# A load moved to another queue, a fetch moved ahead and a token shift rewritten, in the mixer of a hybrid decoder layer

## The chip, the cores and the metric

The kernel runs on one core of one Trainium2 chip. The metric is the device time of one execution in microseconds; the time of a kernel is the median of several runs. The profile is one execution, taken by the hardware profiler: TensorE (PE, with its weight loads as PEld), VectorE (DVE), ScalarE (ACT), GpSimd (POOL) and SyncE (SP), which here only issues DMAs.

## The reference

One decoder layer in float32, with 1024 tokens of 1024 channels: a SwiGLU half-step, a mixer, a SwiGLU half-step, each between two RMS norms. The mixer projects the normed input with one matrix and feeds three branches: RWKV-7 time mixing, sliding-window attention and cross-attention into 256 memory tokens; their outputs are gated, added and projected.

The change concerns the RWKV branch. Its 14 blocks of 128 projected channels go through the token shift:

```
p_prev = pad(p, one token)[:-1]
p = p + (p_prev - p) * mu          # mu: one number for each channel
r, k, v, wd, ad, gd = split(p)
```

From these come a decay, and vectors a and b, and then the recurrence over the tokens for 8 heads of 64 channels:

```
sa = state @ a_t
state = state * w_t + sa * b_t + v_t * k_t
y_t = state @ r_t
```

## The kernel before, in words

**Layout.** Activations lie with channels on the 128 partitions and tokens along the free axis. Tokens are worked in two halves of 512 (`TH`), the size of a PSUM bank. Every large product is done three times (`mm3`, lines 374 to 379): weight and input are each split into a rounded high part and a rest (float32r), and high times high, high times rest and rest times high are added in one bank. A weight strip is loaded by SyncE (`raw`, line 291, five buffers), its high part is made by ScalarE (line 300) and its rest by VectorE (line 302). `prefetch` makes up to eight such operands ahead of their use.

**Who sets the order.** The program is written as a sequence; a planner (the tile framework's scheduler) then lays down a fixed order for every engine from priorities, dependences and its own estimate of costs. `high_priority(offset=...)` moves what stands in it ahead: `lead` is 300, `urgent` is 1000. `issue_after` and `keep_in_program_order` fix an order by hand. Each engine and each DMA queue then takes its instructions strictly in that order, and waits at one whose inputs or buffers aren't ready. A pool with `bufs=2` has two buffers; the third user waits until the first is released, which for a tile that is stored to DRAM means until its store is complete.

**Stages of the mixer.**

1. `rwkv_prep` (line 1002): for each of four pairs of heads the blocks k, r and v are projected (16 times 3 matmuls for a block over both halves) and shifted by `rwkv_block` (line 953); before them come the blocks 12 (`low`) and 13 (`gd`). Four of the 14 blocks (`MIX_FIRST`) were projected already beside the first half-step and wait in `raw` tiles. A `raw` tile has eight columns ahead of its 1024 tokens, the last of them zero, so that columns 7 onward are the tokens shifted by one. For the other ten blocks ScalarE copies both banks into `raw` (line 963). Then VectorE subtracts (line 965) and multiplies and adds (line 966). The results go on to the decay, the norm of the keys (`normed`, `head_sums`, bank name `ss`), the products of keys (`gram`, bank name `ab`) and the planes that are stored in `pk_d` for each chunk of 64 tokens.
2. `win_pair` (line 1407): seven pairs of the other input blocks (attention and gates), each pair in seven products (`b11`, `b21`, `t2`, `t1`, `t3`, `b22`, `t4`) over sums of inputs and sums of weights, which are added in the banks `px`, `py` and `pz`. A pair fills two output tiles, `first` and `second`, of a pool with two buffers; VectorE (line 1433) or ScalarE (lines 1436 and 1438) writes their four halves, and SyncE stores them (line 1455). The half of `second` that the product `t3` gives is read from `px`, into which `t4` is added afterwards.
3. Beside the first pair, `rwkv_invert` (line 1146) inverts, on VectorE, the two triangular 32 by 32 blocks on the diagonal of each of the 128 matrices of 64 by 64, and stores them in `inv_d` (line 1162) and one of them turned in `turn_d` (line 1165).
4. Beside the fifth and sixth pair, `rwkv_corner` (line 1167) makes the remaining 32 by 32 corner: half = up times turned, corner = half times low. Three blocks are loaded with rows and matrices exchanged (line 1177): `up` from `ab_d`, `turned` from `turn_d` and `low` from `inv_d`, each in four DMAs of 128 KB on SyncE with `urgent` priority. Their 512 small matmuls (line 1185) are given out in eight lumps, one behind each product of a pair. ScalarE's queue stores the corner in `inv_d` (line 1191).
5. `chunk_fetch` (line 1193) loads, for one chunk, its planes (`f`, line 1196) and its inverse (`dinv`, two DMAs, line 1198). Those of chunks 0 and 1 are written in the program ahead of the last pair (line 1789), with no priority of their own, after the pool of the corner's tiles has been closed.
6. `rwkv_chain` (line 1201) runs the recurrence over 16 chunks with small matmuls (line 1211). The gate blocks 10 and 11 (`gate_block`, bank name `pgate`) and later the generator `filling` give TensorE work between its steps.

After that come the norm of the branch, both attentions, the branch products and the second half-step.

Of the kernel before, what the change touches and what calls it, by code (L numbers as in the profile page):

```python
# [11 lines left out]
F32 = mybir.dt.float32  # L12
F32R = mybir.dt.float32r
I32 = mybir.dt.int32
ALU = mybir.AluOpType
ACT = mybir.ActivationFunctionType
AXX = mybir.AxisListType.X

P = 128
T = 1024  # L20
TH = 512
# [40 lines left out]
NC_ = T // C  # L62
H = C // 2
# [21 lines left out]
VOFF = {}  # L85
# [146 lines left out]
class Builder:  # L232
# [665 lines left out]
    def mixer_consts(self, cp):  # L898
        nc, io = self.nc, self.io
        V = nc.vector  # L900
        self.lora = cp.tile([P, 512], F32, name="lora")
        nc.scalar.dma_start(self.lora, io["lora"])
        self.g_up = cp.tile([P, 512], F32, name="g_up")
        nc.scalar.dma_start(self.g_up, io["g_up"])
        self.center = cp.tile([P, C], F32, name="center")
        for q in (0, 64):
            V.tensor_scalar(self.center[q : q + 64], self.ident[q : q + 64, q : q + 64], 1.0 / C, None, ALU.subtract)
        self.bones_r = cp.tile([P, P], F32R, name="bones_r")
        bones = self.bones_r.bitcast(F32)
        V.memset(bones, 0.0)  # L910
        for q in (0, 64):
            V.memset(bones[q : q + 64, q : q + 64], 1.0)
        self.gmask = cp.tile([P, 2, C], F32, name="gmask")
        nc.gpsimd.memset(self.gmask, 1.0)
        for q in (0, 64):
            for i, op in ((0, ALU.is_gt), (1, ALU.is_ge)):
                m = self.gmask[q : q + 64, i, :]
                nc.gpsimd.affine_select(m, m, [[1, C]], op, 0.0, base=0, channel_multiplier=-1)
        self.neg_kk = cp.tile([P, NPAIR], F32, name="neg_kk")
        o = VOFF["rwkv_k_k"][0]  # L920
        V.tensor_scalar(self.neg_kk, self.vecs[:, o : o + 4], -1.0, None, ALU.mult)
        self.half_ka, self.half_w0, self.half_a0 = (cp.tile([P, NPAIR], F32, name="half_" + n) for n in ("ka", "w0", "a0"))
        for t, n in ((self.half_ka, "rwkv_k_a"), (self.half_w0, "rwkv_w0"), (self.half_a0, "rwkv_a0")):
            o = VOFF[n][0]
            V.tensor_scalar(t, self.vecs[:, o : o + 4], 0.5, None, ALU.mult)
        self.one_ka = cp.tile([P, NPAIR], F32, name="one_ka")
        V.tensor_scalar(self.one_ka, self.half_ka, -1.0, 1.0, ALU.mult, ALU.add)
        self.half_gb = cp.tile([P, 24], F32, name="half_gb")
        o = VOFF["gate_b"][0]
        V.tensor_scalar(self.half_gb, self.vecs[:, o : o + 24], 0.5, None, ALU.mult)  # L930
        self.ln_half = cp.tile([P, 1], F32, name="ln_half")
        V.memset(self.ln_half, float(np.log(0.5)))
        self.sinks = cp.tile([P, 8], F32, name="sinks")
        nc.scalar.dma_start(self.sinks, io["sinks"])
        self.rope_c = cp.tile([P, 2], F32, name="rope_c")
        nc.scalar.dma_start(self.rope_c, io["rope_c"])
        self.half_pi = cp.tile([P, 1], F32, name="half_pi")
        V.memset(self.half_pi, float(np.pi / 2))
        self.wmask = cp.tile([P, P], F32, name="wmask")
        nc.gpsimd.memset(self.wmask, 0.0)  # L940
        nc.gpsimd.affine_select(self.wmask, self.wmask, [[-1, P]], ALU.is_ge, NEG, base=0, channel_multiplier=1)
        self.is_own = cp.tile([P, P], F32, name="is_own")
        nc.gpsimd.memset(self.is_own, 1.0)
        nc.gpsimd.affine_select(self.is_own, self.is_own, [[1, P]], ALU.is_ge, 0.0, base=0, channel_multiplier=-1)
        before = cp.tile([P, P], F32, name="is_before")
        nc.gpsimd.memset(before, 1.0)
        nc.gpsimd.affine_select(before, before, [[1, P]], ALU.is_gt, 0.0, base=0, channel_multiplier=-1)
        self.is_before = before.bitcast(I32)
        self.gn_eps = cp.tile([P, 64], F32, name="gn_eps")[:, :1]
        V.memset(self.gn_eps, GN_EPS)  # L950


    def rwkv_block(self, f, u, out, within={}):

        nc = self.nc
        if self.first:
            raw = self.first.pop(0)
        else:
            raw = self.raw_tile()
            ps = {h: self.psum("pr") for h in (0, 1)}  # L960
            self.project(self.strip("win", f), u, ps, within)
            for h in (0, 1):
                nc.scalar.copy(raw[:, 8 + h * TH : 8 + (h + 1) * TH], ps[h])
        cur, before = (self.chunked(raw[:, i : i + T], out) for i in (8, 7))
        nc.vector.tensor_tensor(out, before, cur, ALU.subtract)
        self.mixed = nc.vector.scalar_tensor_tensor(out, out, self.vec("rwkv_mu", f), cur, ALU.mult, ALU.add)

    def raw_tile(self, low=False):
        raw = self.rawpool.tile([P, T + 8], F32, tag="rawl" if low else "raw", name="raw", bufs=1 if low else len(MIX_FIRST) - 1)
# [197 lines left out]
    def rwkv_corner(self, pool, ab_d, inv_d, turn_d):  # L1167

        nc = self.nc
        flat = lambda d: d.rearrange("c p q s t -> (c p q) s t")  # L1170
        groups = [slice(g * H, (g + 1) * H) for g in range(P // H)]
        up, turned, low, half, corner = (pool.tile([P, H, H], F32, name="i" + n, bufs=1) for n in ("up", "turned", "low", "half", "corner"))
        urgent = lambda: self.tc.high_priority(offset=self.urgent)
        with urgent():
            for t, d in ((up, flat(ab_d)[:, :H, H:]), (turned, turn_d), (low, flat(inv_d)[:, H:, H:])):
                for g in groups:
                    nc.sync.dma_start(t[g], d[g].rearrange("i s t -> s i t"))
        for w, x, out in ((up, turned, half), (half, low, corner)):
            for a in range(0, H, H // 4):
                if a % (H // 2) == 0:  # L1180
                    ps = self.psum("corner").rearrange("p (i t) -> p i t", t=H)
                with urgent():
                    for i in range(a, a + H // 4):
                        for g in groups:
                            mm = self.tc.keep_in_program_order(nc.tensor.matmul(ps[g, i % (H // 2)], w[g, i], x[g, i], start=True, stop=True))
                    if a % (H // 2):
                        nc.scalar.copy(out[:, a - H // 4 : a + H // 4], ps)
                yield mm
        with urgent():
            for g in groups:  # L1190
                nc.scalar.dma_start(flat(inv_d)[g, :H, H:].rearrange("i s t -> s i t"), corner[g])
# [549 lines left out]
    def mixer(self, u, cp, close_raws, att_d, gate_d, km_d, vm_d):  # L1741
        nc, tc, io = self.nc, self.tc, self.io
        pk_d = tc.dram_tile([NC_, P, NPAIR, 5 * C], F32, name="pk_d")
        ab_d = tc.dram_tile([NC_, NPAIR, 2, C, C], F32, name="ab_d")
        inv_d = tc.dram_tile([NC_, NPAIR, 2, C, C], F32, name="inv_d")
# [18 lines left out]
        with tc.tile_pool(reuse_waits="tile", name="gates", bufs=2) as gp:  # L1764
            out = lambda: gp.tile([P, T], F32, tag="gate", name="att", bufs=2)
# [20 lines left out]
                assert next(lumps, None) is None  # L1786
            chunks = contextlib.ExitStack()
            early = chunks.enter_context(tc.tile_pool(reuse_waits="tile", name="chunks", bufs=2))
            fetched = [self.chunk_fetch(early, c, pk_d, inv_d) for c in (0, 1)]
            self.win_pair(len(WIN_PAIRS) - 1, fs, out, att_d, gate_d)  # L1790
            over.close()
            with chunks, tc.tile_pool(reuse_waits="tile", name="chain", bufs=2) as pool:
# [275 lines left out]
```

## Time and profile before

| | us |
|---|---|
| time, median of three runs | 2256.55 |
| lowest and highest of them | 2255.40, 2257.11 |
| the profiled execution, its time | 2257.27 |
| its span, first to last instruction | 2255.6 |
| granted TensorE clock, mean over the span | 0.997 of full |
| ScalarE busy | 1028.9 |
| GpSimd busy | 58.8 |
| DMA, moved over the span | 431.90 MB |

All positions below are microseconds from the span's start. A row of the order of time gives start, duration, engine, line, operation, output<-inputs, size and count; in brackets stands how long the engine was idle before it and which instruction released it. A row of a list of waits gives the waiter and whom it waited for, then the total in us, the number of waits and the longest. A row of the groups by line gives the operation with its count, shortest/median/longest duration in ns, and the first and last start. SPq and ACTq are DMA issues on the queues of SyncE and ScalarE. The granted clock is a share of TensorE's full clock.

### The profile page before, as it was taken

To read this page: it belongs to the slowest core of one execution; us is meant where nothing else is said; L and a number is where in the kernel's file an instruction comes from. 1 tells how busy PE (TensorE), PEld (TensorE's weight loads), DVE (VectorE), ACT (ScalarE), POOL (GpSimd) and SP (SyncE) were. 2 spreads that over 40 slices of the span, in tenths; PEclk is the share of its full clock that TensorE was granted. 3 is DMA by queue.
4 is the path that set the end of the run, shared out by engine and by line. 5 is a ranking of instruction groups with operands and counts; after the bars stand their busy time and mean duration, and the time that the engine had idled before them with its cause. 6 is when DMAs were issued, how large, how long until landed. Compare 5 with 4: busy or idle time off the path is not lost.

```text
span 2255.6 us, 34511 instructions
## 1 busy us (share of the span) xinstructions
PE 2227.7 (99%) x12304; PEld 1832.2 (81%) x12304; DVE 1642.0 (73%) x2761; ACT 1028.9 (46%) x1933; POOL 58.8 (3%) x114
## 2 busy tenths in 40 slices
PE   8999999999999999999999999999999999999998
PEld 6888888888887788877878887788888888888887
DVE  6988767766698887863667577794898886656576
ACT  6523333454556654444355454444663223345451
POOL 0000000000000000000330000000000000000000
PEclk9999999999999999999999999999999999999999
DMA  8565666686665356464538877564565552347663
GB/s 292 174 202 169 202 210 214 229 294 205 191 210 188 120 150 204 155 169 153 158 95 276 270 252 250 185 202 142 174 214 176 194 189 100 114 164 249 205 196 121
DMA packets 279132, 431.90 MB, mean 191 GB/s; under 512 B 58512, under 2 KB 96912, under 8 KB 278704
## 3 DMA queue, kind: packets, MB, share of 16 engines
q1 hardware_dynamic: 266160, 409.96, 56.0%
q10 hardware_dynamic: 12800, 19.73, 2.7%
q8 instruction: 97, 1.59, 0.3%
q14 instruction: 75, 0.61, 0.1%
HBM read 292.75 MB, written 135.79 MB: 190 GB/s over the span
## 4 chain that ended last, share of the span: by engine, by line
PE 51%; DMA 1%; DVE 1%; ACT 1%; issue 0%; SPq 0%; DVEq 0%; ACTq 0%
PE px L377 4%; PE px L379 4%; PE px L378 4%; PE po L377 3%; PE po L378 3%; PE po L379 3%; PE pgate L377 2%; PE pgate L378 2%; PE pgate L379 2%; PE pz L377 2%; PE pz L379 2%; PE pz L378 2%; PE pb L377 2%; PE pb L378 2%; PE pb L379 2%; PE pw L378 1%
## 5 line engine op out<-in xcount | busy, mean ns | idle before, releaser
L300 ACT CAST w_hi<-w_raw 128x512 fp32r<-128x512 f32 x608 | 376.2, 620 | 725.0 <-PE px L378 189.9
L302 DVE TENSOR_TENSOR w_lo<-w_raw,w_hi 128x512 fp32r<-128x512 f32 x608 | 417.3, 688 | 191.0 <-ACT w_hi L300 171.7
L379 PE MATMUL po<-u,w_lo 128*128 128x512 f32 (+1 forms) x476 | 180.9, 380 | 0.0
L378 PE MATMUL po<-u,w_hi 128*128 128x512 f32 (+1 forms) x476 | 180.9, 380 | 0.0
L377 PE MATMUL po<-u,w_hi 128*128 128x512 f32 (+1 forms) x476 | 180.9, 380 | 0.0
L377 PE MATMUL px<-u,w_hi 128*128 128x512 f32 x380 | 147.9, 389 | 0.8 <-DVE km L1596 0.8
L377 PE MATMUL pz<-u,w_hi 128*128 128x512 f32 x380 | 148.1, 390 | 0.0
L378 PE MATMUL px<-u,w_hi 128*128 128x512 f32 x380 | 147.9, 389 | 0.0
L379 PE MATMUL px<-u,w_lo 128*128 128x512 f32 x380 | 147.8, 389 | 0.0
L379 PE MATMUL pz<-u,w_lo 128*128 128x512 f32 x380 | 147.8, 389 | 0.0
L378 PE MATMUL pz<-u,w_hi 128*128 128x512 f32 x380 | 147.8, 389 | 0.0
L377 PE MATMUL px<-f,w_hi 128*128 128x512 f32 x352 | 137.1, 390 | 0.0
L379 PE MATMUL px<-f,w_lo 128*128 128x512 f32 x352 | 137.0, 389 | 0.0
L378 PE MATMUL px<-f,w_hi 128*128 128x512 f32 x352 | 136.9, 389 | 0.0
L486 DVE TENSOR_TENSOR u<-hid,u 128x512 fp32r<-128x512 f32 x114 | 78.3, 690 | 44.7 <-ACT u L485 43.7
L378 PEld LDWEIGHTS po<-u,w_hi 128*128 128x128 f32 x476 | 89.5, 188 | 17.2
L379 PEld LDWEIGHTS po<-u,w_lo 128*128 128x128 f32 x476 | 89.5, 188 | 17.0
L377 PE MATMUL pgate<-u,w_hi 128*128 128x512 f32 x256 | 103.3, 403 | 0.0
L377 PEld LDWEIGHTS po<-u,w_hi 128*128 128x128 f32 x476 | 89.5, 188 | 16.8
L378 PE MATMUL pgate<-u,w_hi 128*128 128x512 f32 x256 | 101.0, 395 | 0.0
L485 ACT CAST u<-hid 128x512 fp32r<-128x512 f32 x114 | 70.6, 620 | 65.0 <-DMA hid<-form_d 54.2
L379 PE MATMUL pgate<-u,w_lo 128*128 128x512 f32 x256 | 100.3, 392 | 0.0
(453 smaller groups left out, 5162.1 us busy)
## 6 DMA issues: line engine op xcount, KB each, us to landing
w_raw<-in_ffn_in SPq DMA_DIRECT2D x224, 256.0 KB
hid<-form_d SPq DMA_DIRECT2D x154, 256.0 KB
w_raw<-in_win SPq DMA_DIRECT2D x112, 256.0 KB
form_d<-g SPq DMA_DIRECT2D x88, 256.0 KB
w_raw<-ffn_sum_d SPq DMA_DIRECT2D x88, 256.0 KB
form_d<-h SPq DMA_DIRECT2D x66, 256.0 KB
w_raw<-in_ffn_out SPq DMA_DIRECT2D x66, 256.0 KB
first_d<-first SPq DMA_DIRECT2D x48, 256.0 KB
```

What stands on the lines that cost most here:

```text
L300: self.nc.scalar.copy(hi, x)
L302: self.split_last = self.nc.vector.tensor_tensor(lo, x, hi.bitcast(F32), ALU.subtract)
L377: mm(out, wh, xh, start=first, stop=False, **kw)
L378: mm(out, wh, xl, start=False, stop=False, **kw)
L379: self.last_mm = mm(out, wl, xh, start=False, stop=last, **kw)
L485: self.nc.scalar.copy(hi, x)
L486: self.nc.vector.tensor_tensor(lo, x, hi.bitcast(F32), ALU.subtract)
```

## The change

Three edits in the mixer.

- In `rwkv_corner` the block `low` is loaded by GpSimd's queue, in eight DMAs of half the size in place of four on SyncE's. `up` and `turned` stay where they were.
- The fetch of chunks 0 and 1 is given `urgent` priority (1000).
- The token shift is written as out = (1 - mu) * cur + mu * before. A new constant tile `rest_mu` holds 1 - mu. ScalarE writes (1 - mu) * cur into the output, in two halves straight out of the PSUM banks, or in one copy out of `raw` for the four blocks that were projected earlier; VectorE then does one multiply-and-add with the shifted columns. The copies into `raw` stay.

```diff
...
+        self.rest_mu = cp.tile([P, 14], F32, name="rest_mu")
+        o = VOFF["rwkv_mu"][0]
+        V.tensor_scalar(self.rest_mu, self.vecs[:, o : o + 14], -1.0, 1.0, ALU.mult, ALU.add)
...
     def rwkv_block(self, f, u, out, within={}):
         nc = self.nc
+        rest = self.rest_mu[:, f : f + 1]
         if self.first:
             raw = self.first.pop(0)
+            nc.scalar.activation(out, self.chunked(raw[:, 8 : 8 + T], out), ACT.Copy, scale=rest)
         else:
...
                 nc.scalar.copy(raw[:, 8 + h * TH : 8 + (h + 1) * TH], ps[h])
-        cur, before = (self.chunked(raw[:, i : i + T], out) for i in (8, 7))
-        nc.vector.tensor_tensor(out, before, cur, ALU.subtract)
-        self.mixed = nc.vector.scalar_tensor_tensor(out, out, self.vec("rwkv_mu", f), cur, ALU.mult, ALU.add)
+                part = out[:, h * NC_ // 2 : (h + 1) * NC_ // 2] if len(out.shape) == 3 else out[:, h * TH : (h + 1) * TH]
+                nc.scalar.activation(part, self.chunked(ps[h], part), ACT.Copy, scale=rest)
+        self.mixed = nc.vector.scalar_tensor_tensor(out, self.chunked(raw[:, 7 : 7 + T], out), self.vec("rwkv_mu", f), out, ALU.mult, ALU.add)
...
             for t, d in ((up, flat(ab_d)[:, :H, H:]), (turned, turn_d), (low, flat(inv_d)[:, H:, H:])):
                 for g in groups:
-                    nc.sync.dma_start(t[g], d[g].rearrange("i s t -> s i t"))
+                    if t is not low:
+                        nc.sync.dma_start(t[g], d[g].rearrange("i s t -> s i t"))
+                        continue
+                    for a in (0, H // 2):
+                        nc.gpsimd.dma_start(t[g, a : a + H // 2], d[g][a : a + H // 2].rearrange("i s t -> s i t"))
...
-            fetched = [self.chunk_fetch(early, c, pk_d, inv_d) for c in (0, 1)]
+            with tc.high_priority(offset=self.urgent):
+                fetched = [self.chunk_fetch(early, c, pk_d, inv_d) for c in (0, 1)]
             self.win_pair(len(WIN_PAIRS) - 1, fs, out, att_d, gate_d)
```

## The prediction

> **What bounds the kernel now.** I read the page first, then the busy time of each engine by stage, then the list of waits of TensorE, and last the order of time around the one long wait.
>
> ```profile
> span 2255.6 us, 34511 instructions
> PE 2227.7 (99%) x12304; PEld 1832.2 (81%) x12304; DVE 1642.0 (73%) x2761; ACT 1028.9 (46%) x1933; POOL 58.8 (3%) x114
> ```
>
> TensorE works 2227.7 of 2255.6 us. The change takes no matmul away and adds none, so all that it can win is TensorE's idle time, 27.9 us, and time in which its clock was lower. The change touches the mixer only, so the next view is the busy time of the stages that it touches (columns: stretch, its length, then busy time and count of PE, PEld, DVE, ACT and POOL, then granted clock, DMA share, GB/s).
>
> ```profile
> 722.00:900.00 178.00, 175.77 (x1002) 142.27 (x1002) 151.24 (x171) 96.48 (x149) 1.05 (x10) 1.00 0.52 153
> 1000.00:1022.00 22.00, 18.64 (x286) 14.71 (x286) 7.03 (x12) 7.41 (x13) 0.00 (x0) 0.92 0.67 143
> 1060.00:1190.00 130.00, 126.83 (x2029) 104.60 (x2028) 79.54 (x181) 61.82 (x134) 48.08 (x74) 1.00 0.43 134
> ```
>
> The three rows are the preparation of the recurrence (where the token shift runs), the corner, and the chain of chunks. TensorE is idle there for 178.00 - 175.77 = 2.2 us, 22.00 - 18.64 = 3.4 us and 130.00 - 126.83 = 3.2 us. Only in the corner is the clock under 1.00. The waits of TensorE name the causes:
>
> ```profile
> PE px L377 <- DVE att L1433: 3.4, 1, 3.4
> PE z L1211 <- DVE sv L1302: 1.8, 2, 1.1
> PE ss L993 <- DVE n_lo L486: 1.3, 1, 1.3
> ```
>
> The 3.4 us is the corner's, the 1.8 us is two waits in the chain, the 1.3 us one wait in the preparation. The order of time on TensorE at the first:
>
> ```profile
> 1012.57 0.75 PE L1185 MATMUL corner<-iturned,iup 32*32 32x32 f32 x64
> 1016.68 0.65 PE L377 MATMUL px<-mix_form,w_hi 128*128 128x512 f32 x1 [3.36 <-DVE att L1433]
> ...
> 1020.43 0.39 PE L377 MATMUL px<-mix_form,w_hi 128*128 128x512 f32 x1
> 1020.65 0.39 PE L378 MATMUL px<-mix_form,w_hi 128*128 128x512 f32 x1
> ```
>
> ```profile
> 1017.00:1018.00 1.00, 1.00 (x4) 0.71 (x4) 0.00 (x0) 0.43 (x1) 0.00 (x0) 0.50 0.00 0
> ```
>
> After the wait, nine matmuls take 1020.43 - 1016.68 = 3.75 us; the pitch of the next two is 0.22 us, at which nine take 2.0. The granted clock in that stretch is 0.50. So the wait costs 3.36 us of idle time and 1.7 us of slow work, 5.1 us in all. (The Trainium skill, "TensorE: Matmul & The Clock Gate", Part 1 on the clock gate, says that the clock halves after an idle window of about 3.4 us; the trace agrees as far as one wait of 3.36 us can show. By that page a shorter wait would cost no slow work.)
>
> Why was VectorE late? Its own order of time, and the queue of SyncE:
>
> ```profile
> 1012.68 0.69 DVE L1433 TENSOR_TENSOR att<-pz,part 128x512 f32<-128x512 f32 x1 [2.47 <-PE pz L379]
> 1013.29 0.68 DVE L302 TENSOR_TENSOR w_lo<-w_raw,w_hi 128x512 fp32r<-128x512 f32 x1
> ...
> 1015.94 0.68 DVE L1433 TENSOR_TENSOR att<-px,part 128x512 f32<-128x512 f32 x1
> ```
>
> ```profile
> 992.25 5.49 SPq L1177 DMA_DIRECT2D iup<-ab_d  x4
> 997.83 3.53 SPq L1177 DMA_DIRECT2D iturned<-turn_d  x4
> 1001.41 3.69 SPq L1177 DMA_DIRECT2D ilow<-inv_d  x4
> 1005.20 5.36 SPq L291 DMA_DIRECT2D w_raw<-in_win  x4
> 1010.61 12.02 SPq L1455 DMA_DIRECT2D gate_d<-att  x3
> ```
>
> ```profile
> 993.02 0.69 ACT L1436 ACTIVATE att<-px,half_gb 128x512 f32<-128x512 f32 x1
> ```
>
> ```profile
> 1005.90 0.39 PE L379 MATMUL px<-mix_form,w_lo 128*128 128x512 f32 x1
> ```
>
> The operation at 1015.94 (form t3 of the fifth pair, written into the second output tile) had its whole product when the last row ended, at 1006.3, yet it stands behind four other operations. What it could not have had earlier is its output tile: there are two, and the pair before finished the second with the Tanh at 993.02. That tile's store is the first of the three at 1010.61, 17 us after the Tanh, because SyncE's queue held the corner's twelve loads (992.25 to 1005.10) and four weight loads ahead of it. The order on VectorE is fixed beforehand by a planner that knows this dependence, and it put the operation late. TensorE's next product adds into the same bank and waits. So the corner's stall is, by this reading, a store held back in SyncE's queue.
>
> **The change part by part.**
>
> *Low block on GpSimd's queue.* Four loads leave SyncE: 3.69 us. Weight loads and then the store stand 3.7 us earlier, the store at about 1006.9. The twelve loads were also traffic for the same DMA engines:
>
> ```profile
> 1000.00:1010.00 10.00, 10.00 (x106) 8.11 (x105) 2.68 (x5) 3.95 (x7) 0.00 (x0) 1.00 1.08 176
> ```
>
> The share of 1.08 says that the engines were full. If SyncE's issue time was set by them, the low block now competes from 992 with the other eight loads, and twelve equal loads through the same engines end no sooner: the best that is then left is less than 3.7 us, at worst nothing. I take the store some 2 to 3.7 us earlier. (The Trainium skill, "DMA: Bandwidth & Descriptors", "Issuing engines are not separate DMA queues", says that all issuers share the same engines and that another issuer saves only the issue time, usually little; by that rule taken strictly the sum would keep the whole stall and lose its first term, which is the first rival below. Here the issue time is 0.9 us a load in the row, and it is what stands ahead of the store.)
>
> What VectorE needs is that the operation comes directly behind the one at 1012.68 instead of four later. Then it runs from about 1013.3 to 1014.0, and the product starts at 1014.0 where the matmuls of the corner end at 1013.3: 0.7 us of wait stays, and no slow clock. Gain: 3.36 - 0.7 + 1.7 = 4.4 us; the ends are 0 and 5.1.
>
> GpSimd pays with eight issues. It has nothing else to do, and the block is first read at 1025.36:
>
> ```profile
> POOL gz L1222 <- DMA dinv<-inv_d: 202.4, 1, 202.4
> ```
>
> ```profile
> 1025.36 0.75 PE L1185 MATMUL corner<-ilow,ihalf 32*32 32x32 f32 x64
> ```
>
> No issue from GpSimd is in this trace. The nearest rows are SyncE's loads of the same block, 0.9 us for double the size. From 992 to 1025 there are 33 us, 4.1 us for each of eight. At SyncE's price for each the block is issued by 999; I take this value and cost the part at nothing, covered by that slack. Past 4.1 us each, TensorE waits.
>
> *Token shift.* The groups by line:
>
> ```profile
> L965 DVE TENSOR_TENSOR r<-raw x8: 1215/1222/1227, 733.2 to 873.0; 128x1024 f32<-128x1024 f32 x8
> ```
>
> ```profile
> L966 DVE SCALAR_TENSOR_TENSOR r<-r,vecs,raw x8: 1280/1285/1286, 734.4 to 874.3; 128x1024 f32<-128x1024 f32 x8
> ```
>
> ```profile
> L963 ACT COPY raw<-pr x20: 564/588/595, 749.5 to 869.9; 128x512 f32<-128x512 f32 x20
> ```
>
> Fourteen blocks lose a subtraction of 1.22 us on VectorE (17 us). Ten of them gain two copies of 0.59 on ScalarE (11.8 us), the four first blocks one copy of the whole width, about 1.2 by the same row. ScalarE is busy 96.48 of 178.00 us in this stage, VectorE 151.24, so the work goes where there is room; 112 of 178 stays under VectorE's share. On the path of TensorE it only counts at the waits, 2.2 us in all, of which 1.3 is one:
>
> ```profile
> 772.94 1.23 DVE L965 TENSOR_TENSOR k<-raw 128x1024 f32<-128x1024 f32 x1 [1.73 <-ACT raw L963]
> ```
>
> This subtraction for k starts when ScalarE's copy arrives, and k leads to n_lo, for which TensorE waits 1.3 us. Without it the chain is 1.22 us shorter and, for the second scaled copy behind the raw one, 0.6 us longer: 0.6 to 1.2 us earlier. The other 0.9 us are small waits of the same kind. I take 1.2 us for the stage; ends: 2.2, and 0.6 lost if ScalarE's extra copies delay a Tanh that frees a bank. The banks of the blocks are read 1.2 us longer, while a block of 48 matmuls at 0.22 takes 10.6 us and there are two pairs of banks: nothing. New is also one small VectorE operation for the constants, far from any wait: nothing.
>
> *Chunks fetched first.*
>
> ```profile
> 1055.87 0.37 SPq L1196 DMA_DIRECT2D f<-pk_d  x1
> ```
>
> ```profile
> 1039.47 2.16 ACTq L1191 DMA_DIRECT2D inv_d<-icorner  x2
> ```
>
> ```profile
> 1050.69 0.39 PE L377 MATMUL pgate<-u,w_hi 128*128 128x512 f32 x1
> ...
> 1055.67 0.39 PE L378 MATMUL pgate<-u,w_hi 128*128 128x512 f32 x1
> ```
>
> Now the first chunk is fetched at 1055.87, behind the last pair's weights. Its data are complete once the corner is stored, whose last issues begin at 1039.47, so the fetches can stand more than 10 us earlier. TensorE is full until the chain starts, and an earlier chain alone wins nothing. But between 1050.69 and 1055.67 the planner spent eleven gate matmuls (2.4 us at 0.22) in the last pair, and the chain lacks them at its end, where TensorE waits 1.8 us. If the chain's first products take that place, those waits go. Bounds 0 and 2.0 us; I take 1.0. Six DMAs (two planes and four inverse blocks) move ahead of weight loads and stores on SyncE. Twelve loads held that queue for 12.9 us in the corner without TensorE waiting for a weight, so six cost nothing there; the cover is the planned lead of the weights. If the inverse's fetch waits for the corner's store, weights and stores are queued behind it.
>
> Sum: 4.4 + 1.2 + 1.0 = 6.6 us. The profiled execution took 2257.27 us (a span of 2255.6 and 1.67 around it), 0.72 above the median of three, 2256.55. 2257.27 - 6.6 = 2250.67, less 0.72 gives 2250.0 us.
>
> **The rivals.**
>
> *The stall stays.* The DMA engines are the limit, or the planner keeps the order on VectorE, and the store's delay just shrinks. For it: the share of 1.08. Against it: the queue's place is won anyway. The other two parts remain: 1.2 + 1.0, 2256.55 - 2.2 = 2254.4 us. Without those it is 2256.5.
>
> *GpSimd is too slow (slower).* TensorE takes its work in a fixed order, so a late low block stops it at the fifth corner step. With 6 us for each issue the eight end at 992 + 48 = 1040, 14.6 us after 1025.36, with 1.7 us of slow clock behind. The rest of the gain, 6.6, is set against it: 2256.55 + 16.3 - 6.6 = 2266.3 us. It costs from 4.1 us each and makes the kernel slower than before from about 4.8 (38 us, 4.9 late and 1.7 slow). For it: nothing in the trace shows the price. Against it: SyncE's 0.9. (The Trainium skill, "SBUF — State Buffer", section on the two separate sides, adds that VectorE's two-port modes can starve GpSimd's descriptors; no run here shows it.)
>
> *The fetch holds SyncE.* The fetch of the inverse stands ahead of the stores and waits for the corner's store; an output tile is late again, as in the corner, with a wait of 3.4 and slow work of 1.7 in the last pair. That gives back 5.1: 2256.55 - 6.6 + 5.1 = 2255.1 us.
>
> *Not as said:* the chunk tiles may lie where the corner's lay, so that the fetch comes hardly earlier. Then the 1.0 us is missing: 2251.0, within the forecast.
>
> **How the numbers follow.** Forecast 0.55, stall stays 0.25, GpSimd too slow 0.08, fetch holds the queue 0.07, another new wait of a reordered plan 0.05. What a measurement here tells from no change is 0.2%, 4.5 us, so faster means below 2252.0. The forecast's ends are 2247.3 (5.1 + 2.2 + 2.0 = 9.3 gained) and about 2253; most of it is faster: 0.50. Same takes the forecast's rest, the stall that stays and the held fetch: 0.37. Slower: 0.13, from GpSimd and the reordered plan. The range for 8 in 10 reaches from 2247.3 over the stall that stays, without the small terms and with 1 us of new waits, to 2257.5.
>
> **What would show it.** Right: the wait for att in the corner under 1 us with a clock of 1.00 behind it, the first store on SyncE before 1009, the wait of ss gone, fewer gate matmuls ahead of the chain. Wrong: TensorE waiting for the low block, a wait for an output tile elsewhere in the pairs, or VectorE still placing that operation behind four others.

## The result, and the profile after

The changed kernel takes 2261.38 us, the median of ten runs (2259.95 to 2263.78). The kernel before takes 2256.48 in its ten (2255.17 to 2258.43). The ratio is 1.0022, with a 95% interval of 1.0013 to 1.0032: 4.9 us slower, where 6.6 us of gain were forecast. The profiled execution of the changed kernel took 2263.78, 2.4 above its median.

The changed kernel's lines are shifted: the corner loads `up` and `turned` in 1183 and `low` in 1186, its matmuls are 1194; planes are fetched in 1205, inverses in 1207; the chain's matmuls are 1220; VectorE writes a pair's output in 1442, and 1464 stores it.

The page of the changed kernel, span and busy times:

```profile
span 2262.1 us, 34543 instructions
...
PE 2228.6 (99%) x12304; PEld 1831.3 (81%) x12304; DVE 1628.0 (72%) x2748; ACT 1045.1 (46%) x1957; POOL 64.4 (3%) x122
```

TensorE is idle for 33.5 us, 5.6 more than before. VectorE gave up 14 us, where the prediction had 17, and ScalarE took 16, as the edit says. Busy time by stage of the changed kernel, columns as in the prediction:

```profile
722.00:900.00 178.00, 175.78 (x1000) 141.87 (x1001) 136.92 (x159) 111.14 (x170) 1.53 (x10) 1.00 0.50 154
1000.00:1022.00 22.00, 19.70 (x209) 15.81 (x207) 10.10 (x16) 7.86 (x14) 3.98 (x7) 1.00 0.67 156
1070.00:1200.00 130.00, 121.43 (x2006) 100.62 (x2005) 81.70 (x182) 63.09 (x134) 46.30 (x70) 1.00 0.40 123
```

Idle time is 2.2 us in the preparation (2.2 before), 2.3 in the corner (3.4) and 8.6 in the chain (3.2, in this stretch too). The loss is in the chain. The changed kernel's waits of TensorE, with those of other stages left out:

```profile
PE z L1220 <- DVE sv L1311: 7.1, 6, 1.3
...
PE px L377 <- DVE att L1442: 2.3, 1, 2.3
PE ab L1119 <- DVE bk L1103: 1.6, 1, 1.6
```

The wait for `ss` is gone, and one for `ab`, a little later in the same preparation, has its place. The corner's wait is 1.1 us shorter and still there. The chain's two waits are now six.

Where each stands can be read off TensorE's own positions. At the first matmul on the low block the changed kernel is 1.1 us behind the kernel before (which has it at 1025.36):

```profile
1026.46 0.75 PE L1194 MATMUL corner<-ilow,ihalf 32*32 32x32 f32 x64
```

The path to it has three steps. In the first 60 us this execution lost 2.2, a stretch that differs by up to 2.6 between profiles of kernels that are the same there. Between 496 and 664 us, in the second product of the first half-step, it lost 1.5, which will need an experiment. In the corner it won 2.6 (1.1 of idle time and, in this execution, some 1.6 of slow clock). Behind the corner the chain's 5.4 are lost, and 1.1 + 5.4 = 6.5 is the whole difference of the spans.

SyncE's queue around the corner, in the changed kernel:

```profile
995.93 5.32 SPq L1183 DMA_DIRECT2D iup<-ab_d  x4
1001.35 4.58 SPq L1183 DMA_DIRECT2D iturned<-turn_d  x4
1006.03 0.66 SPq L291 DMA_DIRECT2D w_raw<-in_win  x1
```

```profile
1008.46 5.81 SPq L291 DMA_DIRECT2D w_raw<-in_win  x3
1014.32 9.41 SPq L1464 DMA_DIRECT2D gate_d<-att  x3
```

The low block's 3.7 us are gone from the queue, and the store has not moved: from the first load of `up` to the store it was 1010.61 - 992.25 = 18.36 us, and now it is 1014.32 - 995.93 = 18.39. Four weight loads stand between, and the queue halts at them: they wait for one of the five weight buffers, which the work in progress frees at its own pace. VectorE at the same place, and GpSimd's eight issues (the first two and the last two):

```profile
1018.58 0.69 DVE L1442 TENSOR_TENSOR att<-px,part 128x512 f32<-128x512 f32 x1 [0.91 <-DMA gate_d<-att]
```

```profile
995.26 0.83 POOL L1186 DMA_DIRECT2D ilow<-inv_d  x1 [132.45 <-ACT att L1445]
1001.45 0.66 POOL L1186 DMA_DIRECT2D ilow<-inv_d  x1 [5.36 <-issue]
...
1019.24 0.66 POOL L1186 DMA_DIRECT2D ilow<-inv_d  x1 [3.29 <-issue]
1021.95 0.66 POOL L1186 DMA_DIRECT2D ilow<-inv_d  x1 [2.05 <-issue]
```

The first row shows the release directly: VectorE waits for the output tile's store. It now has one operation between this one and the write of `pz` at 1016.38, where it had four; by this reading the planner's order follows the store as far as the planner can foresee it, and the store's landing is the limit. GpSimd needs 27.3 us for its eight issues, 3.4 each, and gives out the last 3.9 us before the block is first read.

The queue of SyncE at the early fetch, and VectorE behind it:

```profile
1044.39 0.38 SPq L1205 DMA_DIRECT2D f<-pk_d  x1
...
1048.37 15.14 SPq L291 DMA_DIRECT2D w_raw<-in_win  x6
1063.57 0.42 SPq L1464 DMA_DIRECT2D gate_d<-att  x1
```

```profile
1067.72 0.69 DVE L1442 TENSOR_TENSOR att<-px,part 128x512 f32<-128x512 f32 x1 [0.91 <-DMA gate_d<-att]
```

The fetch did move, from 1055.87 to 1044.39. But this is the corner's picture once more, in the last pair: six weight loads of 15 us stand ahead of the pairs' store, which goes at 1063.57, and the same operation of VectorE (form t3, into the second output tile) waits for it. In the kernel before the same store went eleven microseconds earlier:

```profile
1052.42 0.42 SPq L1455 DMA_DIRECT2D gate_d<-att  x1
```

There five weight loads stood ahead of it, for 9 us. The fetch itself does not hold the queue: its six issues are out in 3.9 us. The longest halt, 9.6 us, is that of the sixth weight load, whose buffer VectorE frees only at 1063.2.

TensorE does not wait here. Its gate matmuls in this stretch, counted by the group of the bank `pgate` between 1040 and 1072:

```profile
L377 PE MATMUL pgate<-u,w_hi x13: 388/389/389, 1051.8 to 1068.2; 128*128 128x512 f32 x13
...
L378 PE MATMUL pgate<-u,w_hi x12: 389/389/389, 1052.0 to 1067.7; 128*128 128x512 f32 x12
...
L379 PE MATMUL pgate<-u,w_lo x12: 389/389/389, 1055.2 to 1067.9; 128*128 128x512 f32 x12
```

Thirty-seven gate matmuls run ahead of the chain, where eleven did. Thirty of them stand in one row from 1061.59 on, and the product that needs VectorE's operation above follows at 1068.47, as that operation ends. They cover the late tile, 26 more at 0.23 us, 6 us. The chain has 96 of them in all and takes six for most of its 16 steps. Five steps in a row, from 1135.9 on, have none, and there it waits; in the kernel before every step has some.

### The profile page after: what moved, and what is told of

Read it like the earlier page. It is cut to its first block, busy times and chain, and to the rows that moved or that the text cites. A ratio compares the mean times of both kernels' runs of the same rounds, so it can differ in the third digit from the quotient of the medians.

```text
span 2262.1 us, 34543 instructions
## 1 busy us (share of the span) xinstructions
PE 2228.6 (99%) x12304; PEld 1831.3 (81%) x12304; DVE 1628.0 (72%) x2748; ACT 1045.1 (46%) x1957; POOL 64.4 (3%) x122
## 4 chain that ended last, share of the span: by engine, by line
PE 91%; DVE 5%; DMA 2%; ACT 1%; issue 1%; SPq 0%; DVEq 0%; ACTq 0%
PE px L377 9%; PE px L378 9%; PE px L379 9%; PE po L377 6%; PE po L378 6%; PE po L379 6%; PE pz L377 4%; PE pz L379 4%; PE pz L378 4%; PE pgate L377 2%; PE pgate L379 2%; PE pgate L378 2%; PE pr L377 2%; PE pr L378 2%; PE pr L379 2%; PE pb L377 2%
```

## The experiments

The theory from the two traces: the early fetch costs the time, because it stands ahead of the pairs' stores on SyncE, the planner then fills the wait for the late output tile with gate matmuls, and the chain lacks them. The rivals: GpSimd's issues disturb the transfers or VectorE; the token shift's extra work on ScalarE costs; the earlier first chunk itself makes the chain slower. Each time is a median, compared with the kernel before on the same chip.

**Each edit alone.** First the low block, without the other two edits:

```diff
-                    nc.sync.dma_start(t[g], d[g].rearrange("i s t -> s i t"))
+                    if t is not low:
+                        nc.sync.dma_start(t[g], d[g].rearrange("i s t -> s i t"))
+                        continue
+                    for a in (0, H // 2):
+                        nc.gpsimd.dma_start(t[g, a : a + H // 2], d[g][a : a + H // 2].rearrange("i s t -> s i t"))
```

> Only the low block on GpSimd's queue. Theory A (the fetch with its priority is what costs, by the gate matmuls that it makes the planner spend ahead of the chain): the corner's wait is 2.3 us without slow clock as in the changed kernel, the chain waits as before (1.8 to 2 us), time 2.7 us below before, about 2253.8. Rival B (the eight issues of GpSimd, 2.6 to 4 us apart, disturb the loads around the corner): at or above before.

Measured: 2255.60 against 2257.09, ratio 0.9990 (0.9981 to 0.9999). The rival of GpSimd's disturbance, at or above the kernel before, falls, if narrowly; the 2253.8 of the theory was missed too. The waits of this kernel:

```profile
PE px L377 <- DVE att L1437: 2.3, 1, 2.3
PE z L1215 <- DVE sv L1306: 1.6, 2, 0.9
PE ss L993 <- DVE n_lo L486: 1.2, 1, 1.2
```

The gain of 1.5 is the 1.1 us of shorter wait in the corner, and nearly nothing else. Here the slow clock stayed.

The token shift alone (the hunks of `rest_mu` and `rwkv_block`):

```diff
...
-        self.mixed = nc.vector.scalar_tensor_tensor(out, out, self.vec("rwkv_mu", f), cur, ALU.mult, ALU.add)
...
+        self.mixed = nc.vector.scalar_tensor_tensor(out, self.chunked(raw[:, 7 : 7 + T], out), self.vec("rwkv_mu", f), out, ALU.mult, ALU.add)
```

> Only the token shift and its constant tile. Theory A: within 1 us of before (TensorE's waits in the preparation sum to 2.2 us in both kernels). Rival C (the shift and its constant cost the 2 to 3.7 us by which the changed kernel's profile is behind already at the start of the mixer): 2 to 3 us above before, 2258.5 to 2260, and the same lag at the start of the mixer.

Measured: 2258.21 against 2257.09, ratio 1.0005 (0.9996 to 1.0013). The median is 1.1 us worse, not more than the runs can tell from nothing. The wait for `ss` turned into one for `ab`, as in the whole change:

```profile
PE ab L1119 <- DVE bk L1103: 1.5, 1, 1.5
```

The early fetch alone:

```diff
-            fetched = [self.chunk_fetch(early, c, pk_d, inv_d) for c in (0, 1)]
+            with tc.high_priority(offset=self.urgent):
+                fetched = [self.chunk_fetch(early, c, pk_d, inv_d) for c in (0, 1)]
```

> Only the priority of the two fetches. Theory A: six waits of z for sv of 1.24 us, 7 us in all, instead of 1.8; the corner's wait of 3.4 us and its slow clock stay; time 5.4 us above before, about 2262. Rivals B and C: within 1.5 us of before.

Measured: 2263.77 against 2257.09, ratio 1.0027 (1.0016 to 1.0038), with the chain's waits of the whole change:

```profile
PE z L1211 <- DVE sv L1302: 7.3, 6, 1.3
```

So one line of the three edits makes all of the loss. The distances of the three ratios from one, -0.0010, +0.0005 and +0.0027, add up to the 0.0022 of the whole.

**Two edits without the fetch.** Low block and token shift:

```diff
-            with tc.high_priority(offset=self.urgent):
-                fetched = [self.chunk_fetch(early, c, pk_d, inv_d) for c in (0, 1)]
+            fetched = [self.chunk_fetch(early, c, pk_d, inv_d) for c in (0, 1)]
```

> The changed kernel without the fetch's priority. Theory A: the chain waits under 2.2 us, time 2.7 us below before, about 2253.8 and 7 to 8 us below the changed kernel. Rival C: 2256 to 2257, since the shift's cost stays.

Measured: 2256.73 against 2257.09, ratio 0.9998 (0.9989 to 1.0006). Without the fetch the change is worth nothing that can be measured, in either direction. The theory's 2253.8 was missed; the rival in that expectation, that a cost of the shift stays, was right, and is taken up again below.

**The early fetch off SyncE's queue.** All three edits, the first two chunks fetched by GpSimd's queue with the same priority:

```diff
-        S = self.nc.sync
+        S = self.nc.gpsimd if c < 2 else self.nc.sync
```

> The changed kernel, with the fetches of chunks 0 and 1 as urgent as there, but on GpSimd's queue. Theory A, made narrower (the fetches cost because they stand on SyncE's queue ahead of the output stores, so that the planner thinks the last pair's output tile late and spends 30 more gate matmuls there): the gate matmuls ahead of the chain fall back to 11, the waits of z to 1.6 to 2 us, time 6 us below the changed kernel, 2256 to 2257. Rival D (an early first chunk itself changes the chain or loads the DMA engines): the six waits of 1.24 us stay, 2261 to 2263.

Measured: 2257.00 against 2256.87, ratio 0.9999 (0.9990 to 1.0008). The loss is gone while the fetch stays urgent, so an early chunk does not itself slow the chain: that rival falls, and the gate matmuls ahead of the chain are eleven again. The waits:

```profile
PE px L377 <- DVE att L1442: 2.5, 1, 2.5
PE z L1220 <- DVE sv L1311: 1.7, 2, 0.9
```

The chain waits 1.7 us where the kernel before waits 1.8. Fetching the chunks first gained nothing here either: the first chunk's planes are fetched at 1024.22, and still the chain's first product stands 39.41 us behind the first read of the low block, as in the kernel before (39.45).

**The stores ahead instead.** The whole change, and the pairs' stores urgent as well:

```diff
-            nc.sync.dma_start(gate_d[f - 24] if f >= 24 else att_d[ATT_ROW[f]], t)
+            with self.tc.high_priority(offset=self.urgent):
+                nc.sync.dma_start(gate_d[f - 24] if f >= 24 else att_d[ATT_ROW[f]], t)
```

> The changed kernel with its fetches on SyncE as they are, and only the pairs' output stores given the priority 1000 too. Theory A narrowed: the stores no longer wait behind fetches and weights, so both the 30 extra gate matmuls and the corner's wait of 2.3 us go: 2261.4 - 5.5 - 2.3 = 2253.6. Theory A in its first form (the weight loads behind the fetches are what is late): the chain's waits stay at 7 us, only the corner's goes, 2259. Rival D: the same, 2259.

Measured: 2253.37 against 2256.87, ratio 0.9985 (0.9976 to 0.9994). Neither the chain nor the corner waits as before, with the fetch still on SyncE: it is the store's place in that queue that decides. Seven gate matmuls run ahead of the chain. By what estimate the planner had put the store behind a sixth weight load is not on record. The two stages:

```profile
1000.00:1030.00 30.00, 30.00 (x495) 23.99 (x494) 13.61 (x21) 12.72 (x22) 4.53 (x7) 1.00 0.61 142
1070.00:1200.00 130.00, 127.21 (x1941) 105.31 (x1941) 85.51 (x186) 61.82 (x128) 44.26 (x66) 1.00 0.44 135
```

The same edit of the store in the kernel before, with none of the three:

> The kernel before, all twelve corner loads on SyncE, and only the pairs' output stores given the priority 1000. If the corner's wait of 3.4 us and the slow clock behind it are a store held back in SyncE's queue, they go: 2256.5 - 5.1 = 2251.4. If they come from late weights or from the traffic of the small loads, the wait stays over 2 us and the time is within 2 us of before.

Measured: 2251.41 against 2256.87, ratio 0.9976 (0.9966 to 0.9985), the fastest of all. Corner and queue:

```profile
1000.00:1022.00 22.00, 22.00 (x340) 17.76 (x339) 6.55 (x10) 8.49 (x14) 0.00 (x0) 1.00 0.58 111
```

```profile
994.18 2.57 SPq L1456 DMA_DIRECT2D gate_d<-att  x2
996.85 3.77 SPq L1177 DMA_DIRECT2D iup<-ab_d  x4
1000.72 3.88 SPq L1177 DMA_DIRECT2D iturned<-turn_d  x4
1004.64 3.60 SPq L1177 DMA_DIRECT2D ilow<-inv_d  x4
```

```profile
1009.08 0.69 DVE L1433 TENSOR_TENSOR att<-px,part 128x512 f32<-128x512 f32 x1 [1.65 <-PE px L379]
```

The stores go ahead of all twelve loads, the operation of VectorE waits for its product alone, and TensorE never stops at a clock of 1.00. The prediction's cause of the corner's stall is shown; its remedy, by moving the low block, was the wrong one.

Then the low block's move on top of this:

```diff
+                    for a in (0, H // 2):
+                        nc.gpsimd.dma_start(t[g, a : a + H // 2], d[g][a : a + H // 2].rearrange("i s t -> s i t"))
...
+            with self.tc.high_priority(offset=self.urgent):
+                nc.sync.dma_start(gate_d[f - 24] if f >= 24 else att_d[ATT_ROW[f]], t)
```

> The kernel before with the pairs' stores urgent (e7) and, beside it, the low block on GpSimd's queue. Theory that the corner's wait is the held store alone: the store is already early, so the low block's move has nothing left to win, and the time is e7's, 5.5 us under the kernel before, within 1 us. Rival, that the four loads on SyncE cost something of their own (the weights behind them): 1 us or more under e7. Third, that GpSimd's slow issues now come late for the fifth corner step: a wait for ilow and a time over e7 by that wait.

Measured: 2252.26 against 2256.77, ratio 0.9979 (0.9971 to 0.9988), no better than with the store's edit alone. Once the store is not held, the move has nothing left to win.

**One more gate block for the chain.** The whole change, with 48 more gate matmuls in the chain's reserve (the expectation says 24; a block has 48):

```diff
-GATES_EARLY = 12
+GATES_EARLY = 13
```

> All three edits, with thirteen of the sixteen blocks of gate matmuls given to the chain in place of twelve. Theory that the chain's 7.1 us of waits come from gate matmuls spent ahead of it, so that its last chunks have none: with 24 more of them in reserve the waits for sv fall to under 2 us and the time falls by 5 us to about that of e5, the same as the kernel before. Rival, that the early fetch itself slows the chain's steps whatever stands between them: the waits stay above 5 us and the time stays at 1.002 of the kernel before.

Measured: 2264.21 against 2256.77, ratio 1.0028 (1.0016 to 1.0040). The expectation is half missed. The chain's waits are gone, as the theory says, and the time is no better. Waits of the two attentions behind the chain, and three stretches of chain and attention:

```profile
PE pv L101 <- DVE sc L135: 4.2, 1, 4.2
PE sc L101 <- DVE pt L169: 2.0, 1, 2.0
```

```profile
1070.00:1200.00 130.00, 128.67 (x2040) 105.98 (x2039) 78.36 (x177) 61.23 (x134) 46.78 (x70) 1.00 0.43 132
1200.00:1320.00 120.00, 120.00 (x613) 102.55 (x612) 80.02 (x147) 55.20 (x126) 1.96 (x3) 1.00 0.83 277
1320.00:1450.00 130.00, 123.81 (x654) 97.15 (x653) 99.78 (x234) 62.99 (x207) 0.00 (x0) 0.96 0.71 235
```

The chain's stage is idle for 1.3 us in place of 8.6; the attentions are idle for 6.2 us (0.8 in the whole change) with a clock of 0.96, which over 130 us is another 5. This execution took 2266.70; the three of the six with a mean clock of 0.997 or 0.998 took 2260.87 to 2263.00, about the time of the whole change. By this reading the thirteenth block was the attentions' filler. The reserve is one pot, and what the last pair spends too much is missing at its bottom, wherever that is put.

**The constant's place.** In every kernel with the token shift, apart from those of this experiment's end, the matmuls of the second product of the first half-step are a little slower. It ends 60 us before the first block is shifted. The groups of this product between 490 and 670 us, in the kernel with low block and shift:

```profile
L377 PE MATMUL po<-u,w_hi 128*128 128x512 f32 x198 | 77.5, 392 | 0.0
...
L378 PE MATMUL po<-form,w_hi 128*128 128x512 f32 x64 | 25.0, 391 | 0.0
L377 PE MATMUL po<-form,w_hi 128*128 128x512 f32 x63 | 24.9, 395 | 0.0
L379 PE MATMUL po<-form,w_lo 128*128 128x512 f32 x63 | 24.7, 393 | 0.0
```

In the kernel before each has a mean of 389 ns; over the 784 matmuls of all six groups this makes some 1.5 us. The order of the instructions is the same. What differs is that the new constant, 56 bytes on each partition, moves the tiles behind it. The first attempt pads it to 128 bytes, with low block and shift:

```diff
-        self.rest_mu = cp.tile([P, 14], F32, name="rest_mu")
+        self.rest_mu = cp.tile([P, 32], F32, name="rest_mu")[:, :14]
```

> Low block on GpSimd and token shift, no urgent fetch (as in the run of these two edits, 2256.7), with the new constant tile padded from 56 to 128 bytes a partition, so that the tiles behind it lie at the same place within 128 bytes as in the kernel before. If the place is what slows about a hundred matmuls of the first half-step from 0.226 to 0.24 us, they are back at 0.226 and the time falls by 1.5 us, to 2255.2, the time of the low block alone. If the slower matmuls come from the changed order or from chance, they stay.

Measured: 2257.14 against 2256.87, ratio 0.9999 (0.9990 to 1.0008), and the matmuls are as slow:

```profile
L377 PE MATMUL po<-form,w_hi 128*128 128x512 f32 x64 | 25.2, 394 | 0.0
```

The place within 128 bytes is not it. The second attempt moves nothing: the constant goes into columns of an existing tile that were never used, low block and shift as before:

```diff
...
-        self.gn_eps = cp.tile([P, 64], F32, name="gn_eps")[:, :1]
+        spare = cp.tile([P, 64], F32, name="gn_eps")
+        self.gn_eps, self.rest_mu = spare[:, :1], spare[:, 32:46]
...
```

> Low block on GpSimd and the new token shift, as in e4 and e8, but 1 - mu is kept in fourteen unused columns of the tile that holds the norm's epsilon, so that no tile of the kernel lies elsewhere than before. Theory that the place of the first half-step's input tiles costs the time: the 72 to 95 matmuls at 0.24 us of the second ffn product stage fall back to the 2 to 4 of the kernel before, and the time is e4's and e8's less 1.4 us: about 1.6 us under the kernel before. Rival, that something else of the shift slows them (the instruction added at the start, or another order): they stay above 60, and the time stays within 0.5 us of the kernel before.

Measured: 2254.99 against 2256.77, ratio 0.9990 (0.9981 to 0.9999), and the matmuls are fast again:

```profile
L377 PE MATMUL po<-form,w_hi 128*128 128x512 f32 x64 | 24.9, 389 | 0.0
```

The instructions are those of the kernel with the padded constant; only the one that makes the constant stands a few lines later at the start of the program. So it is the place of the tiles that costs the 1.5 us. Why one place is slower than another stays open.

**All three edits, mended.** Stores urgent and the constant in the spare columns:

```diff
...
+        self.gn_eps, self.rest_mu = spare[:, :1], spare[:, 32:46]
...
+            with self.tc.high_priority(offset=self.urgent):
+                nc.sync.dma_start(gate_d[f - 24] if f >= 24 else att_d[ATT_ROW[f]], t)
```

> All three edits with the pairs' stores urgent (e6) and 1 - mu in the unused columns of the epsilon's tile. Theory that the place of the tiles costs e6 its last 1.4 us: about 4.9 us under the kernel before, against 3.5 for e6 and 5.5 for e7. Rival: as e6, 3.5 under. Neither theory has it faster than e7, since the wait of the corner and the waits of the chain are gone in e7 already without the three edits.

Measured: 2252.62 against 2256.77, ratio 0.9979 (0.9970 to 0.9988): 4.15 us under, a little short of the 4.9 expected. A new wait, of 0.8 us, is as large as what is missing:

```profile
PE corner L1194 <- DMA ilow<-inv_d: 0.8, 1, 0.8
```

TensorE reaches the low block earlier in this kernel, at 1021.85, and GpSimd is then late: its seventh load lands at 1022.86, and TensorE goes on at 1022.90. The three edits, at their best, do not beat the one edit of the store.

## Why the prediction was wrong, step by step

- **Chunks fetched first, the step that failed.** The prediction put it as "six cost nothing there; the cover is the planned lead of the weights", with bounds of 0 and 2.0 us of gain and no loss. It cost 6.7 us alone. The lead of the weights did cover the weights; what was not covered was the store behind them. The third rival, the fetch that holds SyncE, named the place and the consequence, an output tile late again in the last pair, and had a chance of 0.07. It was wrong in two things. It let the fetch itself wait, for the corner's store; the six issues were out in 3.9 us, and what halts is the weight loads between them and the output tile's store. And the wait does not show where the tile is late, since gate matmuls fill it, but at the chain's end, where they are then missing. That its price, 5.1 us, is near the 5.4 by which the chain's idle time grew is luck: it was made of a wait and slow work that did not come. The prediction also said that fewer gate matmuls would run ahead of the chain. There were 37, not 11.
- **The gain of 1.0 from an earlier chunk** did not come: with the fetch off SyncE's queue the chain starts no earlier and waits 1.7 us against 1.8.
- **The low block, 4.4 us forecast.** The cause of the stall was right, shown by the urgent stores. The step "weight loads and then the store stand 3.7 us earlier" was wrong: the store is at 18.39 us behind the first load of `up`, 18.36 before, because the weight loads ahead of it wait for buffers. What came is 1.1 us of shorter wait, since VectorE takes the operation one place behind the write of `pz`, where it was four, and then waits 0.9 us for the store.
- **The slow clock, 1.7 of the 4.4.** The prediction took it that a wait of 0.7 us leaves the clock alone, and never came to that: the waits that remain are 2.1 to 2.5 us. In the profile of the changed kernel the slow stretch was missing after 2.30; in the six other profiles with such a wait it was there. That it was missing is luck of where the wait fell, as the last section works out.
- **GpSimd's issues at nothing** held, but by 3.9 us and not by the wide margin that SyncE's 0.9 us gave: 3.4 us each, not far from the 4.1 from which TensorE waits. With everything else mended it did wait, 0.8 us. The price taken for it, SyncE's 0.9 us, was that of an issue; on GpSimd's queue each of these loads starts only when the one before has landed. That rival was underrated.
- **The token shift, 1.2 us.** The wait for `ss` went, as predicted, and one of the same size for `ab` came: the stage is idle for 2.2 us with or without it. The prediction put the new constant at nothing, as far from any wait; the tiles that it moved cost 1.5 us, in a stage that no edit touches.
- **The sum.** Against 6.6 us of gain stand, in the profiles, 2.6 or 1.1 won in the corner with or without the clock, and 5.4 and 1.5 lost. That is a loss of 4.3 to 5.8, around the 4.9 measured.

## What to carry to other kernels

When a transfer is moved ahead in an in-order queue, ask which store stands behind it and who needs that store's buffer. The price of a queue is not only the issue time of what stands in it: a load that waits for a buffer holds everything behind it, and here taking other issues out of the queue moved the store by nothing. Where a planner can fill a wait with spare work, look for the cost where that spare work runs out, and give the urgent place to the store that frees a buffer before moving the loads.

## What the runs showed of the hardware

**GpSimd's queue sent these loads one at a time.** An issue is 0.65 to 0.83 us long, but the next follows after 2.6 to 6.2 us from start to start, for 64 KB of short rows; SyncE gave out the same block in 128 KB loads at 0.9 us each. The eight loads of the changed kernel land 2.3 to 5.9 us after their issue, and each of the other seven starts 0.3 us after the one before has landed (landed at 1001.14, next at 1001.45; at 1005.71, next at 1006.01). The trace shows no semaphore wait between them, and it is the same in the other profiles with these loads. Why is not shown: with the fetch on GpSimd's queue, loads of longer rows did start before the one ahead had landed (the first `dinv` at 1043.82 landed at 1046.18, the second started at 1044.44). The Trainium skill, "DMA: Bandwidth & Descriptors", "Issuing engines are not separate DMA queues", says that another issuer saves only issue time, usually little. The trace agrees, and shows less than that: the store gained nothing.

**The slow clock does not need a wait of 3.4 us.** In the kernel with low block and shift TensorE waited 2.08 us and then had half its clock; the last column but two is the granted clock:

```profile
1016.97 0.79 PE L377 MATMUL px<-mix_form,w_hi 128*128 128x512 f32 x1 [2.08 <-DVE att L1442]
```

```profile
1017.00:1020.00 3.00, 3.00 (x7) 2.42 (x8) 0.51 (x1) 0.72 (x1) 0.86 (x2) 0.50 0.37 135
```

The same followed waits of 2.27, 2.38, 2.45, 2.48 and 2.54 us in other profiles here, and not the 2.30 us of the changed kernel. Each time the slow stretch is about 3.4 us long, but it begins anywhere from some 0.5 us before the wait's end to 1.5 us after it, as the granted clock in narrow stretches tells. The Trainium skill, "TensorE: Matmul & The Clock Gate", Part 1, says that the window of 3.4 us runs freely, which agrees with the shifting start. That an idle window of about 3.4 us is needed, as the prediction quoted, these runs do not bear out.

What decides is where the wait falls. In each of the fourteen profiles the granted clock changes only at whole multiples of 3.413 us from the start of its record (in the changed kernel the record starts at 11.64 and the clock falls at 2254.20, 657 times that far), so the places at which the clock could have changed are known. In the nine profiles with a slow stretch in the corner, the 3.413 us ahead of it hold 1.9 to 3.2 us of TensorE's idle time. In the changed kernel such a place, 1018.57, falls inside the wait (1017.03 to 1019.33) and splits it into 1.5 and 0.8 us, and the clock stays. In the corner 1.9 of 3.4 us were enough, and 1.5 were not.

**Where tiles lie can cost 1.5 us** without any change in the instructions, as the three kernels with the constant show.
